# Down-projection operands made and split during the gate and up products and kept in DRAM as two parts

## Chip, cores and metric

The kernel runs on one core of one Trainium2 chip. The metric is the time of one execution in microseconds on the device: the median of the runs of the kernel before is 2508.19 us (3 runs, 2506.65 to 2509.33).

## The reference

Two transformer blocks follow each other on the same 1024 tokens of 1024 features, all in float32. The part that the change touches is the feed-forward at the end of each block, with 2816 hidden features:

```python
# first block
hn = rms_norm(h, ffn_pre_g)
ff = (jax.nn.silu(hn @ w_gate) * (hn @ w_up)) @ w_down
h = h + rms_norm(ff, ffn_post_g)
...
# second block
h = _rmsnorm(x, norm_ffn[l])
gate, up = jnp.split(h @ w_gu[l], 2, axis=-1)
x = x + (jax.nn.silu(gate) * up) @ w_down[l]
```

Ahead of it stand a convolution and sliding-window attention (first block), and three kinds of attention and a cross attention (second block). Nothing of those changes.

## The kernel before, in words

All activations are held feature-major: tiles of 128 features on the partitions by 512 tokens (a half of the sequence) in the columns. A float32 product is made of three matmuls (`mm3`, L530 to L535): each operand is split into a rounded part `hi` (a cast on ACT) and a low part `lo = x - hi` (a subtraction on POOL or DVE), and hi*hi, hi*lo and lo*hi are summed in PSUM. Weights come from DRAM as one stream of 128x512 pieces; `Weights.quarter` (L147) loads one with four feature tiles of one output column, and `Weights.parted` (L157) splits it with a cast on ACT (L162) and a subtraction on POOL, or on DVE where it is told so (L163).

**Gate and up** (`gated`, L1285). The 22 hidden tiles are taken one after the other; for each, the gate and the up tile of both halves of the tokens come from seven products (Winograd's form of Strassen's algorithm) instead of eight: 7 products x 4 feature tiles x 3 matmuls = 84 matmuls. I call this one hidden tile. For the seven, the weights are subtracted from each other on DVE (`difference`, L166) and split seven times. DVE and ACT take the products out of PSUM; silu(gate) is ACT L1300, the row scale after it POOL L1301, and `store` (L1304) multiplies the up part by it on DVE and sends the float32 tile to DRAM (`zff`, one 256 KB store for each half). The first hidden tiles (4 in the first block, 2 in the second: `NPRE`) are taken product by product, the other 18 + 20 = 38 in a main loop.

**Down** (`lower`, L1373). The hidden tiles are the inner dimension. They are taken in three chunks (`CHUNKS`) of 8, 8 and 6 tiles, and each chunk is once more done with seven products: its inner halves are its first and its last 4 (or 3) tiles, k and k + n, and its token halves are the rows. A chunk has seven stages, `stage` (L1415); each makes the operands of one product (4 or 3 tiles of 512 tokens) and the weights of four pairs of output tiles, and one stage later its 4 x 4 x 3 = 48 (or 36) matmuls run. The operands are x11 and x21 (tile k of the first and the second half of the tokens), x12 and x22 (tile k + n of them), and the sums s1 = x21 + x22, s2 = x11 - s1, s3 = x11 - x21, s4 = x12 + s2. So `seven` loads 4 tiles for each k from `zff`, makes the four sums on DVE (`vec`, L1398) and splits all seven with `parted` (L1391): cast on ACT (L422), subtraction on POOL, or on DVE for k = 1 and 3 (`XDVE`; both L423). Loads from `zff` are issued after `mark`, the last but one store.

**What sets the order.** Each engine works through its own instructions in the order in which a scheduler, at build time, put them; SP's queue (nearly all loads and stores) and POOL's few DMAs are in order too. Tiles come from rings of buffers (`BUFS`): whoever fills a buffer waits until its last reader is done. The rings that matter here are `wq` (weights as they come), `wt` (their differences), `whi` and `wlo` (their parts), `ge` (tiles of the gate stage) and `x` (58 buffers: the operands of the gate products, and then those of the down products).

## Time and profile before

| | |
|---|---|
| median of the runs | 2508.19 us (2506.65 to 2509.33) |
| span of the profiled execution | 2505.9 us |
| what lies around the span | not shown by the page; the median is 2.3 us above the span |
| PE matmul busy | 2372.9 us, 95% of the span, 11892 matmuls |
| DVE, POOL, ACT busy | 1894.8 us (76%), 1641.7 us (66%), 1015.9 us (41%) |
| gate and up products | about 445 to 908 us and 1805 to 2240 us |
| down products | about 908 to 1155 us and 2240 to 2491 us |

Busy time is the union of an engine's instructions. Matmuls overlap each other, so one that lasts 0.39 us starts about 0.23 us after the one before it. Idle time is named by the instruction that came after it and by what that waited for.

### The profile page before, as it was taken

Reading aid. Unit: us, or ns where it says so; the run is one execution under the profiler, and the core shown is the slowest. Engines: PE = TensorE matmul, PEld = TensorE weight load, DVE = VectorE, ACT = ScalarE, POOL = GpSimd, SP = SyncE. Lnnn points to the kernel's source line nnn. Section 1 sums busy time; section 2 is a strip of 40 time slices with the busy share of each in tenths; the row PEclk is TensorE's granted clock in tenths of the full one; section 3 lists DMA queues with packets and bytes.
Section 4 is the critical chain, followed back from the end, with each engine's and each line's share of the span. In section 5 each row is a group of like instructions: output and inputs, shape, how many; then the busy total and the mean of one; then the engine's idle time right before and its main releaser. Section 6 shows DMA issues by size and latency. Waiting matters only on the chain.

```text
span 2505.9 us, 34363 instructions
## 1 busy us (share of the span) xinstructions
PE 2372.9 (95%) x11892; PEld 1908.6 (76%) x11892; DVE 1894.8 (76%) x2784; ACT 1015.9 (41%) x2088; POOL 1641.7 (66%) x1194
## 2 busy tenths in 40 slices
PE   8788999889999999998999999999999999998987
PEld 7666777668888877776878778888878888876766
DVE  7989768999555589999443465676799555579988
ACT  5344754533232243435444353544533222334433
POOL 4657557998766669877522334164489666668885
PEclk9888999999999999999999999999999999999998
DMA  4211126423232233232653448113213222253221
GB/s 144 76 34 34 39 81 213 148 72 118 86 104 80 88 123 105 86 121 95 205 154 113 146 121 280 39 51 95 89 59 105 80 76 88 85 190 103 77 73 67
DMA packets 141421, 259.62 MB, mean 104 GB/s; under 512 B 15712, under 2 KB 28352, under 8 KB 141248
## 3 DMA queue, kind: packets, MB, share of 16 engines
q1 hardware_dynamic: 134512, 235.34, 28.9%
q0 software_dynamic: 6448, 21.91, 2.8%
q8 instruction: 94, 1.54, 0.3%
q14 instruction: 79, 0.65, 0.1%
q10 hardware_dynamic: 288, 0.18, 0.0%
HBM read 188.42 MB, written 68.94 MB: 103 GB/s over the span
## 4 chain that ended last, share of the span: by engine, by line
PE 59%; DVE 14%; issue 3%; POOL 2%; ACT 1%; DMA 1%; SPq 0%; DVEq 0%; POOLq 0%; ACTq 0%
PE p L535 10%; PE p L533 10%; PE p L534 10%; PE mm L533 4%; PE mm L534 4%; PE mm L535 4%; DVE s L1398 2%; PE tp L584 2%; PE low L535 2%; PE low L534 2%; PE low L533 2%; DVE ff L423 2%; DVE wt L174 1%; PE lo L1885 1%; DVE ffacc L1398 1%
## 5 line engine op out<-in xcount | busy, mean ns | idle before, releaser
L163 POOL TENSOR_TENSOR xlo<-wt,xhi 128x512 fp32r<-128x512 f32 (+1 forms) x230 | 358.1, 1575 | 31.7 <-ACT xhi L162 24.0
L163 POOL TENSOR_TENSOR xlo<-wraw,xhi 128x512 fp32r<-128x512 f32 (+1 forms) x204 | 321.3, 1588 | 26.5 <-ACT xhi L162 24.1
L140 POOL TENSOR_TENSOR wlo<-wraw,whi 128x512 fp32r<-128x512 f32 x144 | 205.7, 1437 | 142.1 <-ACT whi L139 120.5
L533 PE MATMUL p<-s,xhi 128*128 128x512 f32 x704 | 278.3, 396 | 1.3 <-DVE u L1292 1.0
L535 PE MATMUL p<-s,xlo 128*128 128x512 f32 x704 | 277.7, 396 | 0.9 <-POOL xlo L163 0.9
L534 PE MATMUL p<-s,xhi 128*128 128x512 f32 x704 | 278.0, 395 | 0.0
L535 PE MATMUL low<-ff,xlo 128*128 128x512 f32 (+1 forms) x628 | 252.9, 403 | 25.2 <-POOL xlo L163 25.2
L534 PE MATMUL low<-ff,xhi 128*128 128x512 f32 (+1 forms) x628 | 251.2, 400 | 6.6 <-DVE ff L423 4.5
L533 PE MATMUL low<-ff,xhi 128*128 128x512 f32 (+1 forms) x628 | 250.5, 400 | 5.5 <-DVE u L1398 3.7
L1301 POOL TENSOR_TENSOR g<-g,rbc 128x512 f32<-128x512 f32 x82 | 116.4, 1421 | 188.2 <-ACT g L1300 188.2
L1300 ACT ACTIVATE g<-g 128x512 f32<-128x512 f32 x82 | 51.9, 633 | 422.2 <-DVE g L1299 413.6
L533 PE MATMUL p<-x,xhi 128*128 128x512 f32 x528 | 210.2, 398 | 5.6 <-ACT early L1300 4.9
L535 PE MATMUL p<-x,xlo 128*128 128x512 f32 x528 | 210.6, 399 | 1.1 <-POOL xlo L163 1.1
L534 PE MATMUL p<-x,xhi 128*128 128x512 f32 x528 | 210.0, 398 | 0.1
L162 ACT CAST xhi<-wt 128x512 fp32r<-128x512 f32 (+1 forms) x248 | 142.6, 606 | 144.0 <-DVE wt L174 103.7
L535 PEld LDWEIGHTS low<-ff,xlo 128*128 128x128 f32 x628 | 122.1, 194 | 59.3 <-POOL xlo L163 32.7
L533 PEld LDWEIGHTS p<-s,xhi 128*128 128x128 f32 x704 | 132.8, 189 | 33.4 <-ACT xhi L162 1.4
L535 PEld LDWEIGHTS p<-s,xlo 128*128 128x128 f32 x704 | 132.6, 188 | 32.6 <-POOL xlo L163 1.8
L534 PEld LDWEIGHTS p<-s,xhi 128*128 128x128 f32 x704 | 132.9, 189 | 31.2
L534 PEld LDWEIGHTS low<-ff,xhi 128*128 128x128 f32 x628 | 122.3, 195 | 35.9 <-DVE ff L423 5.8
L533 PEld LDWEIGHTS low<-ff,xhi 128*128 128x128 f32 x628 | 122.1, 194 | 34.3 <-issue 4.2
L162 ACT CAST xhi<-wraw 128x512 fp32r<-128x512 f32 (+1 forms) x228 | 129.6, 599 | 36.4 <-POOL xlo L163 13.5
(446 smaller groups left out, 6445.9 us busy)
## 6 DMA issues: line engine op xcount, KB each, us to landing
wraw<-wstream SPq DMA_DIRECT2D x408, 256.0 KB, 3.0
ff<-zff SPq DMA_DIRECT2D x88, 256.0 KB, 3.5
zff<-up SPq DMA_DIRECT2D x76, 256.0 KB, 2.0
res<-zres SPq DMA_DIRECT2D x48, 256.0 KB, 5.4
x<-xT SPq DMA_DIRECT2D x32, 256.0 KB, 5.4
zres<-res SPq DMA_DIRECT2D x32, 256.0 KB, 2.0
lqk<-zl POOLq DMA_DIRECT2D x16, 512.0 KB, 6.3
wraw<-wstream SPq DMA_DIRECT2D x32, 192.0 KB, 3.1
```

The costliest lines, as they stand in the source:

```text
L140: self.last_part = nc.gpsimd.tensor_tensor(lo, raw, hi.bitcast(F32), op=ALU.subtract)
L162: self.nc.scalar.copy(hi, raw)
L163: ins = (eng or self.nc.gpsimd).tensor_tensor(lo, raw, hi.bitcast(F32), op=ALU.subtract)
L174: self.nc.vector.tensor_tensor(t, a, b, op=ALU.subtract)
L423: return (eng or nc.gpsimd).tensor_tensor(lo, src, f32(hi), op=ALU.subtract)
L533: nc.tensor.matmul(ps, lhsT=ah, rhs=bh, start=first and i == 0, stop=False)
L534: nc.tensor.matmul(ps, lhsT=ah, rhs=bl, start=False, stop=False)
L535: nc.tensor.matmul(ps, lhsT=al, rhs=bh, start=False, stop=last and i == n - 1)
L584: nc.tensor.transpose(ps[:, tsl(j)], pr[:, c0 + (g + j) * P:][:, :P], ident)
L1300: nc.scalar.activation(t, t, AF.Silu)
L1301: nc.gpsimd.tensor_tensor(t, t, rb_[h], op=ALU.mult)
L1398: nc.vector.tensor_tensor(out, x_, y_, op=op)
```

## The change

In `gated`, a hidden tile is no longer stored as it is. Tiles 2m and 2m + 1 of both token halves are now x11, x21, x12, x22 of one operand index m, so that the inner halves of a chunk are its even and its odd tiles; `quarter` takes its weight tiles in steps of two accordingly. As soon as the four are there, the sums are made on DVE in the gate stage. Each of the seven operands is then put to DRAM in two parts (`put`): ACT rounds it (`hi`), and SP stores that; ACT rounds it once more with the sign turned (`lo` = -hi), a DMA from POOL's queue adds the operand to it in place (`accum_op`, `lo` = x - hi), and SP stores that. `some` lets one such put follow after each of four of the seven products of a hidden tile in the main loop; what is left follows the last product. `lower` then only loads the two parts, two 256 KB loads for each operand tile, and no longer subtracts, adds or splits activations. Weights are subtracted and split as before, but their parts have rings of their own (`phi`, `plo`: 6 buffers each); `ge` goes from 9 to 13 buffers, `wt` from 6 to 5, `wq` from 8 to 7. The loads are now issued after the last weight load of the gate stage (`W.last`). Comments are gone too, and line numbers shift: the rounding of weights is L161 in place of L162, their subtraction L162 in place of L163.

```diff
-BUFS = {'v': 39, ..., 'ge': 9, 'wt': 6, 'wq': 8, ...}
+BUFS = {'phi': 6, 'plo': 6, 'hi': 2, 'lo': 3, 'fs': 2, 'v': 39, ..., 'ge': 13, 'wt': 5, 'wq': 7, ...}
...
-    def quarter(self, mat, k, c0, n=4):
+    def quarter(self, mat, k, c0, n=4, step=1):
...
-        self.order += [(mat, k + i, c0) for i in range(n)] + [None] * (4 - n)
+        self.order += [(mat, k + i * step, c0) for i in range(n)] + [None] * (4 - n)
...
-        hi = self.pool.tile([P, 512], F32R, tag="whi", name=f"xhi{self.made}", bufs=BUFS["whi"])[:, :w]
-        lo = self.pool.tile([P, 512], F32R, tag="wlo", name=f"xlo{self.made}", bufs=BUFS["wlo"])[:, :w]
+        hi = self.pool.tile([P, 512], F32R, tag="phi", name=f"xhi{self.made}", bufs=BUFS["phi"])[:, :w]
+        lo = self.pool.tile([P, 512], F32R, tag="plo", name=f"xlo{self.made}", bufs=BUFS["plo"])[:, :w]
...
+    OPERANDS = ("x11", "s1", "s2", "s3", "x22", "s4", "x12")
...
-        z = dp.tile([NFF, 2, P, HALF], F32, name=nm("zff"))
+        z = dp.tile([NFF // 2, 7, 2, P, HALF], F32, name=nm("zff"))
+        f, due = {}, []
+
+        def put(name, m, t):
+            hi = slot("hi", HALF)("hi", F32R)
+            nc.scalar.copy(hi, t)
+            nc.sync.dma_start(z[m, OPERANDS.index(name), 0], f32(hi))
+            lo = slot("lo", HALF)("lo", F32R)
+            nc.scalar.activation(lo, t, AF.Copy, scale=-1.0)
+            nc.gpsimd.dma_start(lo, t, accum_op=ALU.add)
+            nc.sync.dma_start(z[m, OPERANDS.index(name), 1], f32(lo))
+
+        def ready(i, h, t):
+            f[i, h] = t
+            m = i // 2
+            if i % 2 == 0:
+                if h == 0:
+                    due.append(lambda: put("x11", m, t))
+                return
+            due.append(lambda: put(("x12", "x22")[h], m, t))
+            if any((j, g) not in f for j in (i - 1, i) for g in (0, 1)):
+                return
+            x11, x21, x12, x22 = (f.pop((j, g)) for j in (i - 1, i) for g in (0, 1))
...
+            due.extend((s3, s1, s2, s4))
+
+        def some(n=1):
+            for _ in range(min(n, len(due))):
+                due.pop(0)()
...
         def store(i, h, up_, g):
             nc.vector.tensor_tensor(up_, up_, g, op=ALU.mult)
-            return nc.sync.dma_start(z[i, h], up_)
+            ready(i, h, up_)
...
+            some()
             ps = product("p2", pair, sums)
...
+            some()
             ps = product("p6", pair, sums)
...
+            some()
             ps = product("p5", pair, sums)
...
+            some()
             ps = product("p3", pair, sums)
             with tc.high_priority(offset=EVP):
-                last = store(i, b, tt(ge("up1"), ps, u2, ALU.add), g1)
-            if i == NFF - 2:
-                mark = last
-        return z, mark
+                store(i, b, tt(u2, ps, u2, ALU.add), g1)
+        some(len(due))
+        return z, W.last
...
-        def load(k, h):
-            t = xt("ff")
-            with tc.issue_after(mark.ins):
-                late[0] = nc.sync.dma_start(t, z[k, h])
-            return t
-
-        def parted(t, k):
-            hi, lo = xt("ff", F32R), xt("ff", F32R)
-            ins = split(hi, lo, t, nc.vector if k in XDVE else nc.gpsimd)
-            if k not in XDVE:
-                late[1] = ins
+        def operand(name, m):
+            hi, lo = xt("ff", F32R), xt("ff", F32R)
+            for t, part in ((hi, 0), (lo, 1)):
+                with tc.issue_after(mark.ins):
+                    late[0] = nc.sync.dma_start(f32(t), z[m, OPERANDS.index(name), part])
             return hi, lo
...
-                return [W.quarter(down, n0 + n * row, (2 * q + col) * P, n) for q in Q4]
+                return [W.quarter(down, n0 + row, (2 * q + col) * P, n, 2) for q in Q4]
 
-            def stage(ws, xs, evac, done=None):
-                parts = [parted(t, k) for k, t in enumerate(xs)]
+            def stage(ws, name, evac, done=None):
+                parts = [operand(name, n0 // 2 + k) for k in K]
...
-            x21 = [load(n0 + k, 1) for k in K]
-            x22 = [load(n0 + n + k, 1) for k in K]
-            s1 = [xt("s1") for k in K]
-            for k in K:
-                vec(s1[k], x21[k], x22[k])
-            yield stage(t, s1, ev5)
+            yield stage(t, "s1", ev5)
...
```

**Where instructions move.** POOL in the main loop of the first block's gate stage. `xlo` are low parts of weights, `g` the scale after silu, `oh` a table that is loaded once. Before:

```order
L163 TENSOR_TENSOR xlo_5975<-wt_5972,xhi_5974 128x512
L1301 TENSOR_TENSOR g_810_5800<-g_810_5800,rbc_4462 128x512
L163 TENSOR_TENSOR xlo_5996<-wt_5993,xhi_5995 128x512
L163 TENSOR_TENSOR xlo_6015<-wt_5970,xhi_6014 128x512
L163 TENSOR_TENSOR xlo_6037<-wt_6034,xhi_6036 128x512
L163 TENSOR_TENSOR xlo_6061<-wraw_5966,xhi_6060 128x512
L1301 TENSOR_TENSOR g_818_5892<-g_818_5892,rbc_4618 128x512
```

The same place now; `lo` is the low part of an operand, and L1301 is now the DMA that adds to it:

```order
L1351 TENSOR_TENSOR g_832_5753<-g_832_5753,rbc_4462 128x512
L162 TENSOR_TENSOR xlo_5930<-wraw_5927,xhi_5929 128x512
L1301 DMA lo_6141<-up_798_5462 128x512
L1301 DMA lo_6198<-s_885_6193 128x512
L162 TENSOR_TENSOR xlo_5967<-wt_5964,xhi_5966 128x512
L1301 DMA lo_6252<-s_892_6247 128x512
L162 TENSOR_TENSOR xlo_5988<-wt_5985,xhi_5987 128x512
L162 TENSOR_TENSOR xlo_6014<-wt_5962,xhi_6013 128x512
L1351 TENSOR_TENSOR g_845_5862<-g_845_5862,rbc_4618 128x512
```

Between the same two `g` POOL now has three DMA issues beside the four subtractions, each of which waits for ACT to have written its `lo`.

SP's queue in the same place. Before, two stores for each hidden tile (L1306) stand between the weight loads (L113; `z` is the table of the relative bias):

```order
L113 DMA wraw_6834<-wstream 128x512
L113 DMA wraw_6836<-wstream 128x512
L1153 DMA z_3441<-z2s_6273 128x512
L113 DMA wraw_6949<-wstream 128x512
...
L113 DMA wraw_6970<-wstream 128x512
L1306 DMA zff_4111<-up_882_6464 128x512
L1306 DMA zff_4111<-up_878_6418 128x512
L113 DMA wraw_6994<-wstream 128x512
```

Now:

```order
L112 DMA wraw_6304<-wstream 128x512
L112 DMA wraw_6335<-wstream 128x512
L1298 DMA zff_4111<-hi_6195 128x512
L112 DMA wraw_6337<-wstream 128x512
L1298 DMA zff_4111<-hi_6249 128x512
L1302 DMA zff_4111<-lo_6141 128x512
L1302 DMA zff_4111<-lo_6198 128x512
L1302 DMA zff_4111<-lo_6252 128x512
L112 DMA wraw_6531<-wstream 128x512
L1298 DMA zff_4111<-hi_6296 128x512
L112 DMA wraw_6560<-wstream 128x512
L1302 DMA zff_4111<-lo_6299 128x512
```

Stores of low parts (L1302), each of which waits for POOL's adding DMA to land, now stand directly ahead of weight loads in the same queue.

POOL in the first block's down stage. `ff` are low parts of operands, `ffacc` sums of the output. Before:

```order
L163 TENSOR_TENSOR xlo_9002<-wraw_8737,xhi_9001 128x512
L423 TENSOR_TENSOR ff_8986<-ff_8641,ff_8985 128x512
L163 TENSOR_TENSOR xlo_9006<-wraw_8739,xhi_9005 128x512
L423 TENSOR_TENSOR ff_8994<-ff_8645,ff_8993 128x512
L163 TENSOR_TENSOR xlo_9010<-wraw_8741,xhi_9009 128x512
L423 TENSOR_TENSOR ff_9098<-ff_8761,ff_9097 128x512
L423 TENSOR_TENSOR ff_9106<-ff_8765,ff_9105 128x512
L423 TENSOR_TENSOR ff_9198<-s_1157_8769,ff_9197 128x512
```

Now:

```order
L162 TENSOR_TENSOR xlo_9160<-wraw_9135,xhi_9159 128x512
L162 TENSOR_TENSOR xlo_9164<-wraw_9137,xhi_9163 128x512
L162 TENSOR_TENSOR xlo_9168<-wraw_9139,xhi_9167 128x512
L162 TENSOR_TENSOR xlo_9264<-wt_9239,xhi_9263 128x512
L162 TENSOR_TENSOR xlo_9268<-wt_9241,xhi_9267 128x512
L162 TENSOR_TENSOR xlo_9272<-wt_9243,xhi_9271 128x512
```

Only the weights' subtractions are left between the sums of the output.

## Rows read from the trace of the kernel before

**Rows 1.** First page, engine totals: busy us, share of the span, instructions.
```profile
PE 2372.9 (95%) x11892; PEld 1908.6 (76%) x11892; DVE 1894.8 (76%) x2784; ACT 1015.9 (41%) x2088; POOL 1641.7 (66%) x1194
```
**Rows 2.** Windows: gate main loops (first two), then the two down stages.
```profile
core 0: us, PE busy (x) PEld busy (x) DVE busy (x) ACT busy (x) POOL busy (x), PEclk, DMA share, GB/s
640.00:880.00 240.00, 240.00 (x1043) 194.63 (x1042) 136.75 (x182) 70.76 (x131) 161.88 (x114) 1.00 0.27 88
1920.00:2240.00 320.00, 320.00 (x1384) 259.51 (x1384) 197.13 (x251) 93.03 (x169) 224.75 (x152) 1.00 0.28 94
908.00:1155.00 247.00, 226.03 (x945) 179.17 (x944) 233.82 (x251) 105.25 (x198) 204.91 (x134) 0.97 0.30 96
2240.00:2452.00 212.00, 193.49 (x795) 152.73 (x794) 204.83 (x216) 82.46 (x154) 181.28 (x113) 0.96 0.30 98
```
**Rows 3.** Groups of PE by line, down stage of the first block: busy, mean ns | idle before.
```profile
L535 PE MATMUL low<-ff,xlo 128*128 128x512 f32 x307 | 124.9, 407 | 13.0 <-POOL xlo L163 13.0
L533 PE MATMUL low<-ff,xhi 128*128 128x512 f32 x308 | 124.5, 404 | 1.4 <-DVE u L1398 1.4
L534 PE MATMUL low<-ff,xhi 128*128 128x512 f32 x308 | 124.1, 403 | 2.1 <-POOL ff L423 2.1
L494 PE MATMUL bc<-constr,sum 128*64 128x1 f32 x16 | 1.0, 247 | 4.4 <-DVE sum L448 4.4
```
**Rows 4.** The same groups, down stage of the second block up to its tail.
```profile
L535 PE MATMUL low<-ff,xlo 128*128 128x512 f32 x263 | 107.1, 407 | 12.2 <-POOL xlo L163 12.1
L534 PE MATMUL low<-ff,xhi 128*128 128x512 f32 x264 | 107.0, 405 | 4.5 <-DVE ff L423 4.5
L533 PE MATMUL low<-ff,xhi 128*128 128x512 f32 x264 | 105.6, 403 | 1.8 <-DVE res L1398 1.8
```
**Rows 5.** Waits in the first block's down stage: us in total, times, longest.
```profile
ACT xhi L162 <- DVE wt L174: 52.7, 14, 7.9
ACT ff L422 <- DVE s L1398: 41.8, 18, 6.2
```
**Rows 6.** Groups of POOL and of DVE, first block's down stage.
```profile
L423 POOL TENSOR_TENSOR ff<-ff,ff 128x512 fp32r<-128x512 f32 x22 | 37.8, 1728 | 1.9 <-issue 1.9
L423 POOL TENSOR_TENSOR ff<-s,ff 128x512 fp32r<-128x512 f32 x18 | 27.9, 1555 | 14.7 <-ACT ff L422 14.7
...
L423 DVE TENSOR_TENSOR ff<-ff,ff 128x512 fp32r<-128x512 f32 x18 | 27.3, 1523 | 0.0
L423 DVE TENSOR_TENSOR ff<-s,ff 128x512 fp32r<-128x512 f32 x15 | 19.5, 1299 | 1.4 <-ACT ff L422 1.4
```
**Rows 7.** Groups of POOL, DVE and ACT, main loop of the first gate stage (640 to 880 us).
```profile
L1301 POOL TENSOR_TENSOR g<-g,rbc 128x512 f32<-128x512 f32 x25 | 32.5, 1299 | 72.2 <-ACT g L1300 72.2
L1145 POOL DMA_DIRECT2D oh<-oh x4 | 2.3, 582 | 0.0
...
L1305 DVE TENSOR_TENSOR up<-up,g 128x512 f32<-128x512 f32 x24 | 30.1, 1293 | 0.4
...
L162 ACT CAST xhi<-wt 128x512 fp32r<-128x512 f32 x50 | 28.5, 615 | 0.0
```
**Rows 8.** Windows at the start of the main loops, first and second block.
```profile
560.00:640.00 80.00, 80.00 (x346) 64.71 (x346) 69.47 (x78) 25.65 (x47) 66.22 (x41) 1.00 0.36 119
1840.00:1920.00 80.00, 80.00 (x349) 64.92 (x348) 73.27 (x69) 24.59 (x44) 69.77 (x46) 1.00 0.25 83
```
**Rows 9.** DMA issues of the whole span: times, size of one, median us to landing.
```profile
zff<-up SPq DMA_DIRECT2D x76, 256.0 KB, 2.0
oh<-oh POOLq DMA_DIRECT2D x2, 256.0 KB, 3.2
aq<-zfq POOLq DMA_DIRECT2D x4, 512.0 KB, 9.2
```
**Rows 10.** Windows with the most DMA traffic outside the stages above.
```profile
375.00:405.00 30.00, 30.00 (x154) 24.29 (x154) 20.60 (x33) 11.57 (x23) 19.10 (x18) 1.00 0.72 244
1500.00:1550.00 50.00, 50.00 (x269) 41.27 (x268) 24.63 (x54) 14.34 (x31) 26.77 (x26) 1.00 0.96 329
```

More of the change, by code (lines that the diff above doesn't have):

```diff
@@ L30 @@
 BYDVE = (3,)
-XDVE = (1, 3)
 POSTPOOL = (0, 1, 2, 4, 5, 6)
@@ L1288, in gated, with fs, s3, s1 @@
         b = 1 - a
-        z = dp.tile([NFF, 2, P, HALF], F32, name=nm("zff"))
+        z = dp.tile([NFF // 2, 7, 2, P, HALF], F32, name=nm("zff"))
[8 more added lines that the diff above has]
+            nc.sync.dma_start(z[m, OPERANDS.index(name), 1], f32(lo))
+        def fs(name):
+            return slot("fs", HALF)(name)
+        def ready(i, h, t):
[9 more added lines that the diff above has]
+            x11, x21, x12, x22 = (f.pop((j, g)) for j in (i - 1, i) for g in (0, 1))
+            s = {}
+            def s3():
+                d = tt(fs("s3"), x11, x21, ALU.subtract)
+                put("s3", m, d)
+            def s1():
+                tt(x21, x21, x22, ALU.add)
+                put("s1", m, x21)
+            def s2():
+                s[2] = tt(fs("s2"), x11, x21, ALU.subtract)
+                put("s2", m, s[2])
+            def s4():
+                put("s4", m, tt(fs("s4"), s[2], x12, ALU.add))
+            due.extend((s3, s1, s2, s4))
+        def some(n=1):
+            for _ in range(min(n, len(due))):
+                due.pop(0)()
         def tt(out, x_, y_, op):
@@ L1479, in seven @@
             b11 = weights(0, 0)
-            x11 = [load(n0 + k, 0) for k in K]
-            yield stage(b11, x11, ev1)
+            yield stage(b11, "x11", ev1)
             b12 = weights(0, 1)
             t = [W.difference(b12[q], b11[q]) for q in Q4]
-            x21 = [load(n0 + k, 1) for k in K]
-            x22 = [load(n0 + n + k, 1) for k in K]
-            s1 = [xt("s1") for k in K]
-            for k in K:
-                vec(s1[k], x21[k], x22[k])
-            yield stage(t, s1, ev5)
+            yield stage(t, "s1", ev5)
             b22 = weights(1, 1)
-            for k in K:
-                vec(s1[k], x11[k], s1[k], ALU.subtract)
             t2 = [W.difference(b22[q], t[q], t[q]) for q in Q4]
-            yield stage(t2, s1, ev6)
-            for k in K:
-                vec(x11[k], x11[k], x21[k], ALU.subtract)
-            yield stage([W.difference(b22[q], b12[q], b12[q]) for q in Q4], x11, ev7, 3)
-            x12 = [load(n0 + n + k, 0) for k in K]
+            yield stage(t2, "s2", ev6)
+            yield stage([W.difference(b22[q], b12[q], b12[q]) for q in Q4], "s3", ev7, 3)
             b21 = weights(1, 0)
@@ L1502, in seven @@
                     before_last()
-            yield stage([W.difference(t2[q], b21[q], t2[q]) for q in Q4], x22,
+            yield stage([W.difference(t2[q], b21[q], t2[q]) for q in Q4], "x22",
                         adder(2, ALU.subtract), 2)
-            for k in K:
-                vec(s1[k], s1[k], x12[k])
-            part = stage(b22, s1, adder(1), 1)
+            part = stage(b22, "s4", adder(1), 1)
             def first_half():
@@ L1515, in seven @@
             tail = end and not fresh_all and TAIL
-            last = stage(b21, x12, adder(0), -1 if tail else 0)
+            last = stage(b21, "x12", adder(0), -1 if tail else 0)
             if end and ahead:
```

3 lines of the change are left out of this document (2 added, 1 removed).

## Prediction, made before the change was run

> **What bounds the kernel now.** The first page comes first: PE's matmuls are busy for 95% of the span [rows 1], so an engine beside PE matters only where PE waits for it. The windows show where that is. In the main loops of the two gate stages PE is never idle, and 1384 matmuls take 320.00 us: 0.2312 us each [rows 2]. At that rate the 945 matmuls of the first down stage would take 218.5 us; they take 247, 28.5 more. The 795 of the second one, up to its tail, would take 183.8 us and take 212, 28.2 more. So 56.7 us are lost in the two down stages, and this is the stretch that the change relieves.
>
> What PE waits for there is in its groups by line [rows 3, 4]. In the first block: 13.0 us for POOL's low part of a weight, 2.1 for POOL's low part of an operand, 1.4 for a sum on DVE, 4.4 for a sum of squares at the end; in the second 12.1 (12.2 with all), 4.5 for DVE's low part of an operand, 1.8 for a sum. Together 39.4 us of idling. The other 17 us are mostly the clock, which falls after such waits: the granted clock is 0.97 and 0.96 of full speed over these windows, 0.03 x 247 + 0.04 x 212 = 15.9 us, while it is 1.00 in the gate loops [rows 2].
>
> Most waits are for weights, which the change leaves where they are. But why they are late is one step further back: POOL and DVE are busy for 83% and 95% of the first down window [rows 2], ACT waits 52.7 us for differences of weights that DVE has not made yet and 41.8 for sums of operands [rows 5], and POOL's `xlo` comes after ACT's `xhi`. DVE's backlog, then POOL's, reaches PE.
>
> **What goes from the down stages.** Each layer has 11 operand indices x 7 = 77 splits: 77 casts on ACT, 42 subtractions on POOL (k = 0 and 2; some 1.65 us each [rows 6]: 69 us) and 35 on DVE (some 1.4 us [rows 6]: 49 us), and 44 sums on DVE (priced at 1.29, the two-input DVE row of the gate stage [rows 7]: 57 us). DVE is left with 234 - 106 = 128 us of the 247, POOL with 205 - 69 = 136. Neither is then close to full. I take all waits for `xlo` and for `ff` to end: 13.0 + 12.1 + 2.1 + 4.5 = 31.7 us. The clock's part goes with them in proportion, 31.7 / 39.4 x 15.9 = 12.8 us. **Down: -44.5 us.** The sums of squares and of the output stay.
>
> **What the down stages get.** Two loads in place of one load and a split for each operand: 154 loads of 256 KB a layer instead of 44, and no engine between DRAM and PE. They fill buffers of the `x` ring, 58 deep, some six stages ahead. In the first layer, with 48 weight loads (a quarter of a MB or less), 16 residual loads and 8 weight pieces for the next block, that is some 58 MB in 219 us, 266 GB/s; the stage moves 96 GB/s now [rows 2]. The traffic has been as high as 329 GB/s over 50 us with PE fully busy [rows 10], so I expect it to pass, but with less room: weights stand in SP's queue behind operand loads, `wq` and `wt` have one buffer fewer, and the parts of weights have 6 buffers each instead of sharing 8. New waits lie between 0 and the 31.7 us that I took off; with DVE and POOL half free I take a quarter. **+8 us.**
>
> **What the gate stages get.** A hidden tile has 84 matmuls, 19.4 us. The window of 240 us holds 1043 / 84 = 12.4 of them [rows 2]. For each, on average, come 3.5 puts and two sums:
> - POOL: 161.88 / 12.4 = 13.0 us, plus 3.5 DMA issues. An adding DMA is in no row; the nearest is POOL's issue of a plain DMA, 0.58 us [rows 7]. 15.1 us of 19.4.
> - DVE: 136.75 / 12.4 = 11.0, plus 2 x 1.29 = 13.6 us.
> - ACT: 70.76 / 12.4 = 5.7, plus 7 casts of 0.62 [rows 7] = 10.0 us.
> - SP: 5 more stores, issue time alone; a store lands in 2.0 us [rows 9].
> - Transfers: 5 stores and 3.5 additions of 256 KB are 2.2 MB more in 19.4 us, 115 GB/s beside the 88 at a share of 0.27 [rows 2]; the share goes to some 0.6, or 0.77 if an addition counts twice.
>
> So every engine stays under PE's 19.4 us, and that spare time is the cover; where it is gone is the start of the loops. There DVE is busy for 69.5 and 73.3 of 80 us [rows 8], and four hidden tiles would add 10.7: 80.2 and 84.0. The lower bound is nothing, the upper is the first rival's. I take 4 us a layer, the overflow in the fuller of the two windows. **+8 us.** The last puts run beside the first down chunk, and only the last chunk reads them: nothing. Ordering loads after the last weight load, and even and odd tiles instead of halves, cost nothing: the host lays out the weights, and the transfers keep their size.
>
> **Sum.** -44.5 + 8 + 8 = -28.5 us. It is made from one profiled execution with a span of 2505.9 us, 2.3 under the median of 2508.2; I apply it to the median: 2479.7, **2480 us**.
>
> **Rivals.** *A, POOL becomes the bound of the gate stages (slower).* POOL has 19.4 - 13.0 = 6.4 us to spare for each hidden tile, and it is not all usable: its order is fixed, and it stands 72.2 us in 240 before the scale after silu [rows 7], 5.8 us a tile. If 1 us of that cannot be filled, 3.5 issues fit as long as one takes under 1.54 us. If an issue has to sit out a DVE operation, 0.58 + 1.29 = 1.87 us [rows 7], POOL is 1.15 us over in each of 38 tiles: +44 in place of my +8, 2516 us, and 133 us more for each further us of an issue. Against it: the plain issues took 0.58 us beside a busy DVE, and POOL arrives later at silu, so most of the standing goes.
>
> The Trainium skill, page "SBUF — State Buffer", sections "SBUF: two separate sides" and "A bandwidth-pool intuition that's wrong (but worth ruling out)", speaks against the change here: POOL writes the descriptors of its own DMAs itself, a DVE copy in a mode that takes the port both share locks it out, and a DMA of some 620 ns then took some 3100. By that figure an issue would cost 3.1 us and POOL would need 13.0 + 3.5 x 3.1 = 23.9 us a tile, an estimate of 4.5 x 38 = 170 us lost from that page. The page says it of copies and casts, not of two-input operations, which are most of DVE's work in this loop; the trace's four issues agree with its undisturbed figure.
>
> *B, the addition lands late (slower).* A low part passes ACT's cast (0.62), POOL's issue (0.58), the landing L, SP's store and its landing (some 0.4 + 2.0), 3.6 + L in all, through a ring of three, and the store blocks SP's queue meanwhile, weight loads behind it. 3.5 of them take 3.5 / 3 x (3.6 + L) us a tile. POOL's DMAs landed in 3.2 us for 256 KB and 9.2 at most for 512 KB [rows 9]; from L = 13 the ring is slower than PE, at 14 it costs 1.1 us x 38 = 42 in place of my 8: 2514 us, and more if the puts bunch.
>
> *C, the change does not do what it says for weights.* PE waits for `xlo`, and those splits stay, with fewer buffers. If only half of the down term comes off, with the new waits in it: 2508.2 - 22.3 + 8 = 2494 us.
>
> *D, the down stages become bound by transfers.* At 244 GB/s, a rate that the trace shows at a share of 0.72 [rows 10], 58 MB take 238 us instead of 219: 19 us return in the first layer and some 15 in the second, which has no reloads: 2508.2 - 44.5 + 34 + 8 = 2506 us.
>
> **How the numbers follow.** My forecast, 2462 to 2496 by its own bounds (the whole down term less little, or twice the new costs), gets 0.47; C 0.18; A 0.17; B 0.09; D 0.09. About 0.2%, 5 us, is what a measurement of this kernel can tell from no change. Forecast and C are faster, but for a corner of C (0.64 with a little of D); D and the edges of C and A fall within 0.2% (0.09); A, B and a part of D are slower (0.27). The range holds the forecast, C, D and the near parts of A and B: 2458 to 2530 us.
>
> **What would show it.** Right: in the down windows the granted clock is 1.00, PE's idle before `low` falls from the 35 us of [rows 3, 4] (without the sums of squares) to under 10, DVE is busy for half; the gate loops keep 0.231 us a matmul; POOL's adding DMA is issued in about 0.6 us and lands in 3 to 6. Wrong: gaps before p products behind POOL's `xlo` or `g` (A), stores of `lo` in SP's queue waiting over 10 us and weights late behind them (B), `xlo` still at the head of PE's waits in the down stages (C), or PE there waiting for a DMA of `ff` at a share near 1 (D).

## The result, and the profile after

The changed kernel takes **2548.8 us** (median of 4 runs, 2546.8 to 2551.8) against 2508.7 of the kernel before on the same chip: a ratio of **1.0161, 95% interval 1.0146 to 1.0175**. It is 40 us slower, where 28 us faster was forecast, and outside the range. The profiled execution has a span of 2549.7 us, 43.8 more than the one shown of before.

Where that went is read by stretches, from the first to the last matmul of the gate products (`p`) and of the down products (`low`); the last column is an experiment told below, the change without its addition.

| stretch, us | before | after | difference | without the addition |
|---|---|---|---|---|
| start to the end of the first gate stage | 908.0 | 934.8 | +26.8 | 909.6 |
| first down stage | 247.0 | 231.0 | -16.0 | 214.8 |
| second block up to its gate stage | 650.1 | 665.4 | +15.3 | 665.9 |
| second gate stage | 435.5 | 481.3 | +45.8 | 434.4 |
| second down stage | 250.6 | 223.7 | -26.9 | 216.1 |
| rest | 14.6 | 13.4 | -1.2 | 13.7 |

So the two down stages gave 42.9 us, where 36.5 net were forecast, and the two gate stages cost 72.6. Windows of the changed kernel, the four of [rows 2] with the down stages at their new places:

```profile
core 0: us, PE busy (x) PEld busy (x) DVE busy (x) ACT busy (x) POOL busy (x), PEclk, DMA share, GB/s
640.00:880.00 240.00, 231.16 (x983) 183.63 (x983) 201.64 (x196) 109.49 (x205) 184.17 (x149) 0.99 0.70 194
1920.00:2240.00 320.00, 300.72 (x1250) 236.73 (x1250) 293.05 (x255) 135.21 (x253) 228.86 (x188) 0.98 0.63 176
...
935.00:1166.00 231.00, 219.15 (x941) 175.42 (x941) 132.66 (x181) 75.42 (x144) 131.94 (x105) 0.97 0.76 260
...
2312.00:2536.00 224.00, 219.50 (x997) 178.48 (x996) 142.85 (x201) 68.93 (x131) 127.89 (x99) 0.98 0.72 246
```

In the first down stage DVE and POOL are busy for 57% each (95% and 83% before), and PE's groups there, against [rows 3], show no wait for POOL but a new one for transfers:

```profile
L533 PE MATMUL low<-ff,xhi 128*128 128x512 f32 x308 | 122.2, 398 | 1.8 <-DMA ff<-zff 1.8
L534 PE MATMUL low<-ff,xlo 128*128 128x512 f32 x308 | 121.5, 398 | 1.1 <-POOL xlo L162 0.8 <-DVE xlo L162 0.4
L532 PE MATMUL low<-ff,xhi 128*128 128x512 f32 x308 | 120.2, 398 | 8.9 <-DMA ff<-zff 8.9
```

The gate loops were at 1043 and 1384 matmuls with PE never idle; now 983 and 1250 pass in the same time. PE's waits in the two gate stages (428 to 935 us, then 1831 to 2312):

```profile
PE p L534 <- POOL xlo L162: 20.4, 25, 2.5
PE p L532 <- ACT xhi L161: 7.7, 5, 2.6
...
PE p L534 <- POOL xlo L162: 23.0, 17, 4.0
PE p L532 <- ACT xhi L161: 8.5, 6, 3.0
```

These short waits on the parts of weights point to POOL. But POOL is busy for 184.17 us of 240 and 228.86 of 320 (161.88 and 224.75 before), so it is far from full. What has changed most is DVE: from 197.13 to 293.05 us of 320, for fewer matmuls. Two of its groups in the second gate loop before:

```profile
L1299 DVE TENSOR_TENSOR g<-g,rbc 128x512 f32<-128x512 f32 x33 | 23.7, 719 | 1.1
...
L174 DVE TENSOR_TENSOR wt<-wraw,wt 128x512 f32<-128x512 f32 x15 | 12.1, 809 | 0.0
```

Its groups there after the change, and POOL's in the first loop:

```profile
L173 DVE TENSOR_TENSOR wt<-wraw,wt 128x512 f32<-128x512 f32 x15 | 69.6, 4638 | 5.4 <-DMA zff<-hi 3.1 <-ACT xhi L161 2.3
L1349 DVE TENSOR_TENSOR g<-g,rbc 128x512 f32<-128x512 f32 x30 | 60.8, 2027 | 1.0
L1355 DVE TENSOR_TENSOR up<-up,g 128x512 f32<-128x512 f32 x15 | 26.7, 1781 | 0.0
...
L1342 DVE TENSOR_TENSOR u<-u,p 128x512 f32<-128x512 f32 x30 | 20.4, 680 | 0.9
```
```profile
L162 POOL TENSOR_TENSOR xlo<-wt,xhi 128x512 fp32r<-128x512 f32 x45 | 73.8, 1751 | 5.5 <-DMA zff<-hi 3.6 <-ACT xhi L161 1.8
...
L1351 POOL TENSOR_TENSOR g<-g,rbc 128x512 f32<-128x512 f32 x23 | 33.9, 1474 | 24.7 <-ACT g L1350 24.7
L1301 POOL DMA_DIRECT2D lo<-s x18 | 22.8, 1283 | 0.0
L1301 POOL DMA_DIRECT2D lo<-u x12 | 11.5, 962 | 11.8 <-ACT lo L1300 11.0 <-issue 0.6
L1301 POOL DMA_DIRECT2D lo<-up x12 | 10.7, 890 | 13.2 <-DVE wt L173 6.2 <-ACT lo L1300 4.2 <-ACT hi L1297 2.8
```

Read the means. DVE's operations with one input from PSUM (`u<-u,p`) still take 680 ns. Those with both inputs from SBUF, the difference of weights and the row scale, went from 809 and 719 ns to 4638 and 2027. The record of an adding DMA's issue on POOL lasts 0.89 to 1.28 us, not 0.58. (These records overlap their neighbours: counted from the end of the instruction before it, an adding DMA takes 0.87 us of POOL in this loop, and the plain copy of experiment 2 0.55.) POOL's standing before `g`, 72.2 us in [rows 7], is down to 24.7. The timeline of one place, first DVE, then POOL, shows how the two belong together (columns: start, duration):

```profile
709.31 0.69 DVE L1342 TENSOR_TENSOR g<-u,p 128x512 f32<-128x512 f32 x1 [0.30 <-DMA zff<-lo]
710.03 5.32 DVE L1349 TENSOR_TENSOR g<-g,rbc 128x512 f32<-128x512 f32 x1
715.27 0.68 DVE L173 TENSOR_TENSOR wt<-wraw,wraw 128x512 f32<-128x512 f32 x1
```
```profile
708.30 0.88 POOL L1301 DMA_DIRECT2D lo<-up  x1
708.89 1.19 POOL L1301 DMA_DIRECT2D lo<-s  x1
709.46 1.93 POOL L162 TENSOR_TENSOR xlo<-wt,xhi 128x512 fp32r<-128x512 f32 x1
710.70 1.53 POOL L1301 DMA_DIRECT2D lo<-s  x1
711.32 3.47 POOL L162 TENSOR_TENSOR xlo<-wt,xhi 128x512 fp32r<-128x512 f32 x2
716.10 1.29 POOL L1351 TENSOR_TENSOR g<-g,rbc 128x512 f32<-128x512 f32 x1 [1.31 <-ACT g L1350]
```

A row scale of 0.69 us stands for 5.32, as long as POOL goes from one instruction to the next without a pause, and ends 0.56 us after POOL's last one, in its pause. Of DVE operations over 3 us the gate stages have 25 (2 before). The next silu, on ACT, starts only when this one is over.

That such stalls reach PE shows in the second loop. Seven differences of weights take 7.0 to 7.1 us each there, and 20.2 to 20.4 us after the start of each PE has just stood 1.6 us for POOL's low part of a weight: the first one starts at 1961.19, and PE goes on at 1981.36. Over both gate stages, against the run without the addition, PE is idle for 44 us more (70.8 in place of 26.6), and for as many matmuls busy for 28 us more, at a granted clock of 0.97 in both in place of 0.98 and 1.00. That is the 72 us.

Which DVE operations stand can be read from all 19 traces of this case, over the gate stages and for operations of 128x512 float32. The 5665 with one input from PSUM took 0.67 to 0.69 us each, whatever POOL did. The 2207 with both inputs from SBUF that no instruction of POOL's overlapped took 0.67 to 0.70. The 6279 others of these took up to 10.1 us, 1.46 in the mean. Beside one operation of POOL's the longest took 1.81 us, and only such were held up as began after POOL's; the 151 beside one issue of a DMA alone, adding or plain, stayed at 0.67 to 0.70. So a DVE operation with both inputs from SBUF waits for POOL's subtractions and scales, and not for its DMA issues.

### The profile page after: what moved, and what is told of

Read it like the earlier page. It is cut to its first block, busy times and chain, and to the rows that moved or that the text cites. A ratio compares the mean times of both kernels' runs of the same rounds, so it can differ in the third digit from the quotient of the medians.

```text
span 2549.7 us, 35644 instructions
## 1 busy us (share of the span) xinstructions
PE 2394.1 (94%) x11892; PEld 1911.9 (75%) x11892; DVE 1904.9 (75%) x2714; ACT 1096.0 (43%) x2242; POOL 1561.6 (61%) x1264
## 3 DMA queue, kind: packets, MB, share of 16 engines
q8 instruction: 94, 1.54, 0.2%
## 5 line engine op out<-in xcount | busy, mean ns | idle before, releaser
L162 POOL TENSOR_TENSOR xlo<-wt,xhi 128x512 fp32r<-128x512 f32 (+1 forms) x230 | 360.3, 1651 | 136.6 <-ACT xhi L161 116.1
L162 POOL TENSOR_TENSOR xlo<-wraw,xhi 128x512 fp32r<-128x512 f32 (+1 forms) x204 | 298.6, 1541 | 28.7 <-ACT xhi L161 10.8
L534 PE MATMUL p<-s,xlo 128*128 128x512 f32 x704 | 284.5, 406 | 26.1 <-POOL xlo L162 26.1
L532 PE MATMUL p<-s,xhi 128*128 128x512 f32 x704 | 283.3, 402 | 11.6 <-ACT xhi L161 7.1
L533 PE MATMUL p<-s,xhi 128*128 128x512 f32 x704 | 281.4, 400 | 0.0
L532 PE MATMUL low<-ff,xhi 128*128 128x512 f32 (+1 forms) x628 | 244.3, 394 | 13.4 <-DMA ff<-zff 8.9
L533 PE MATMUL low<-ff,xhi 128*128 128x512 f32 (+1 forms) x628 | 246.7, 394 | 1.8 <-DMA ff<-zff 1.8
L534 PE MATMUL low<-ff,xlo 128*128 128x512 f32 (+1 forms) x628 | 245.5, 393 | 1.1 <-POOL xlo L162 0.8
L161 ACT CAST xhi<-wt 128x512 fp32r<-128x512 f32 (+1 forms) x248 | 144.9, 605 | 209.6 <-DVE wt L173 170.8
L1351 POOL TENSOR_TENSOR g<-g,rbc 128x512 f32<-128x512 f32 x82 | 122.5, 1496 | 101.5 <-ACT g L1350 101.4
L173 DVE TENSOR_TENSOR wt<-wraw,wt 128x512 f32<-128x512 f32 (+1 forms) x74 | 145.1, 1962 | 19.7 <-POOL xlo L162 8.4
L1349 DVE TENSOR_TENSOR g<-g,rbc 128x512 f32<-128x512 f32 x82 | 151.6, 1852 | 2.3
L532 PEld LDWEIGHTS low<-ff,xhi 128*128 128x128 f32 x628 | 119.2, 190 | 41.5 <-ACT xhi L161 13.4
L161 ACT CAST xhi<-wraw 128x512 fp32r<-128x512 f32 (+1 forms) x228 | 131.4, 600 | 37.3 <-DMA wraw<-wstream 18.7
```

Of the source, the lines that this page charges most:

```text
L161: self.nc.scalar.copy(hi, raw)
L162: ins = (eng or self.nc.gpsimd).tensor_tensor(lo, raw, hi.bitcast(F32), op=ALU.subtract)
L173: self.nc.vector.tensor_tensor(t, a, b, op=ALU.subtract)
L532: nc.tensor.matmul(ps, lhsT=ah, rhs=bh, start=first and i == 0, stop=False)
L533: nc.tensor.matmul(ps, lhsT=ah, rhs=bl, start=False, stop=False)
L534: nc.tensor.matmul(ps, lhsT=al, rhs=bh, start=False, stop=last and i == n - 1)
```

## The experiments

Lines without a number belong to `put`; medians of before are those of the same chip. "Gates" is the first gate stage plus the second, first to last `p` matmul: 898.7 us before, 987.0 after.

**1. Without the addition.** `-nc.gpsimd.dma_start(lo, t, accum_op=ALU.add)`

> Leaves out the adding DMA: the stored low part is -hi instead of x - hi. Everything else of the change stays. Four theories of the 88 us that the two gate stages lost. Starved DVE: DVE's two-input operations (the row scale, the differences of weights, the product with silu) stand while POOL runs one instruction behind another, and the adding DMAs have filled the pauses that POOL had. Then the pauses return, the mean of the row scale on DVE falls from 2175 ns to under 1000, the two gate stages lose less than 20 us against the kernel before: 2465 to 2485 us. Adding itself: the addition is slow or blocks something as an addition; same result here. Traffic (5 more stores of 256 KB a hidden tile, and the addition): most of it stays, 2530 to 2550 us. Added work (2 sums on DVE and 7 casts on ACT a hidden tile): nothing comes back, 2540 to 2550 us.

2455.3 us against 2507.1 (0.979, 0.9774 to 0.9806): 94 us less than the change, 52 less than before, 10 under the lower end that was expected. Gates 915.0 (16 more than before, since the first one starts 16 us earlier with the 56 matmuls told of below; it ends 1.6 us later), no waits in the down stages. The last column of the table above is this run. Stores, casts and DVE's sums are all still there, and the loops are back at 1043 and 1385 matmuls, so those cost nothing by themselves in the loops. DVE's row scale takes 1093 ns in the first loop, not quite under 1000.

```profile
640.00:880.00 240.00, 240.00 (x1043) 194.62 (x1042) 179.94 (x211) 117.89 (x224) 160.42 (x116) 1.00 0.47 164
1920.00:2240.00 320.00, 320.00 (x1385) 259.70 (x1384) 239.68 (x284) 152.59 (x285) 201.64 (x144) 1.00 0.51 176
```

**2. A plain copy in its place.** `+nc.gpsimd.dma_start(lo, t.bitcast(F32R))`

> The adding DMA becomes a plain copy of the same tile from the same queue of POOL (the stored low part is x instead of x - hi); the order of every engine stays the same. Starved DVE: POOL issues as many DMAs in the same places, so DVE is as starved: the row scale on DVE stays over 1700 ns, 2535 to 2555 us. Adding itself: 2465 to 2490 us. Traffic: the copy moves the same bytes or a little less, 2535 to 2550 us.

2477.0 us (0.9883, 0.9861 to 0.9904): 72 of the 94 us belong to the adding as such, 22 to a DMA on POOL's queue (18 of them in the gate stages). That as many issues starve DVE as much is refuted (the row scale takes 1427 ns). This run has the issue price that the prediction used. The copies are issued in half the time:

```profile
L1301 POOL DMA_DIRECT2D lo<-s x18 | 9.9, 553 | 0.0
L1301 POOL DMA_DIRECT2D lo<-up x12 | 7.2, 600 | 12.5 <-ACT lo L1300 6.3 <-DVE wt L173 6.2
```

**3. The copy from ACT's queue.** `+nc.scalar.dma_start(f32(lo), t)`

> The same copy, but issued from ACT's queue right behind the second cast (the stored low part is x instead of x - hi): traffic and stores as with the copy from POOL's queue, no DMA on POOL. Starved DVE: the row scale on DVE under 1000 ns, 2465 to 2490 us. Traffic: 2535 to 2550 us. Added work: 2535 to 2550 us.

2453.6 us (0.979, 0.9775 to 0.9805), 11 under the expected range, gates 914.9: moving the same bytes costs nothing, at a DMA share of 0.60 and 0.63 in the loops' windows.

**4. A subtraction on POOL.** `+nc.gpsimd.tensor_tensor(lo, t, f32(hi), op=ALU.subtract)` for the second cast and the addition

> The second cast and the adding DMA are replaced by a subtraction on POOL, which computes the same. POOL then works 13.0 + 3.5 x 1.6 = 18.6 us of the 19.4 us of a hidden tile and issues no DMA there. Starved DVE: what counts is that POOL has no pauses, not that it issues DMAs: the row scale on DVE stays over 1500 ns, and the kernel is as slow as the change or slower, 2535 to 2600 us. If it is the issue of a DMA on POOL that stops DVE (and not a dense POOL): the row scale under 1100 ns, 2475 to 2510 us.

2531.5 us (1.0102, 1.0087 to 1.0117), between the two expected ranges, gates 985.1: nearly as slow as the change without any DMA on POOL, but in another way. POOL is full (218.96 of 240 us), the row scale takes 1137 ns, and only 2 of DVE's operations in the gate stages take over 3 us. So a POOL without pauses is not enough for those long stalls; that part of the theory fell.

**5. and 6. Adding DMAs alone, and copies alone, on the kernel before:** 3.5 for each hidden tile, from `rb_[b]` into a ring of three. The scheduler did not leave them there: in experiments 5 to 10 the added operations stand in the first part of each loop, up to 11 a hidden tile (the full adding DMAs in tiles 2 to 13, counted from 0, of 22, the subtractions in 2 to 14), and none after.

```diff
+            lo = slot("lo", HALF)("lo", F32R)
+            nc.scalar.activation(lo, rb_[b], AF.Copy, scale=-1.0)
+            nc.gpsimd.dma_start(lo, rb_[b], accum_op=ALU.add)
```

> The kernel before, with nothing of the change but 3.5 adding DMAs (and the cast ahead of each) for each hidden tile of the two gate loops, 133 in all, from a tile that is always there into a ring of three; their results are read by nobody, no store waits for them. Two theories of why adding costs 72 us more than copying. Issue: the adding DMA holds POOL for 0.9 to 1.3 us in place of 0.57, POOL's subtraction behind it takes some 2.2 us, and DVE's two-input operations wait for both; then it costs time here too, 2525 to 2570 us, DVE's row scale over 1200 ns in place of 713. Landing: the addition lands in 6.4 us instead of 3.8, so stores of low parts block SP's queue and the ring; here nothing waits for it but the ring: 2505 to 2515 us.

> The same with plain copies in place of the adding DMAs. Issue: 0.57 us of POOL each, which fits into the pauses; 2505 to 2520 us. Landing: 2505 to 2512 us.

2543.2 us with adding DMAs (1.0148, 1.0128 to 1.0169), 2515.3 with copies (1.0037, 1.0024 to 1.005), against 2506.0: +37 and +9. No store waits here, so late landing is not needed for the loss. DVE's row scale takes 1157 ns in the first loop, a little under what was expected, and 1538 in the second.

**7. and 8. Half the rows, half the columns** (`lo[0:64, :]`, and `lo[:, 0:256]`, source alike)

> The adding DMAs alone on the kernel before, each over 64 of the 128 partitions (half the rows of 2 KB, half the bytes). If POOL's hold goes with the rows that an adding DMA has to be written out for, the issue takes 0.5 to 0.65 us instead of 1.16 and the kernel 2508 to 2525 us. If it is a fixed price of an adding DMA: 1.0 us and more, 2530 to 2550 us.

> The same with all 128 partitions and 256 of the 512 columns (the same number of rows, half the bytes). If the hold goes with the rows: issue 1.0 to 1.2 us, 2530 to 2550 us. If it goes with the bytes: 0.5 to 0.65 us, 2508 to 2525 us.

2539.5 us (1.0125, 1.0109 to 1.0142) and 2537.3 (1.0117, 1.0101 to 1.0134). The hold is neither by rows nor by bytes: counted from the end of the instruction before it, an adding DMA takes 0.83 to 0.85 us of POOL alone, 0.80 over half the rows and 0.84 to 0.85 over half the columns, and a copy alone 0.52 to 0.53. POOL's issues in the full, the half-row and the half-column run:

```profile
L1308 POOL DMA_DIRECT2D lo<-rbc x133 | 154.5, 1198 | 1.9 <-ACT xhi L162 1.0 <-ACT lo L1307 0.7
```
```profile
L1308 POOL DMA_DIRECT2D lo<-rbc x133 | 155.4, 1331 | 2.7 <-ACT lo L1307 1.8 <-ACT xhi L162 0.9
```
```profile
L1308 POOL DMA_DIRECT2D lo<-rbc x133 | 152.8, 1217 | 8.3 <-ACT lo L1307 5.7 <-PE p L534 2.7
```

**9. and 10. Every second adding DMA only; and a subtraction on POOL in the place of each**

> The adding DMAs alone on the kernel before, full size, but only every second one (66 in place of 133); the casts stay. With the run of half the rows it compares half the bytes in as many DMAs with half the bytes in half as many. If the price is per adding DMA: half the loss of 37 us, 2515 to 2528 us. If the price comes from their density (two or three in a row that shut DVE out): most of it goes, 2505 to 2515 us.

> On the kernel before, in the place of each of the 133 adding DMAs a subtraction on POOL (some 1.6 us each, more of POOL's time than the 1.2 us of an adding DMA's issue). If an adding DMA costs through the time it takes on POOL: more than the 37 us of the adding DMAs, 2545 to 2570 us. If it costs mainly through what it does to DVE's operations and to the subtraction behind it: less, 2510 to 2535 us, with fewer operations of DVE over 3 us than the 41 there.

2525.5 us against 2508.8 (1.0073, 1.0052 to 1.0093): half as many cost half. But they are not half as dense: the scheduler put them into the first seven tiles of either loop, 4.8 a tile in place of some 6.5, so the theory of density was hardly tested. With subtractions 2573.5 (1.0266, 1.0248 to 1.0284): +65, more than the adding DMAs and 3.5 above the expected range, with 5 operations of DVE over 3 us in the gate stages where these have 37. The time that POOL is given counts, then, but it is not all: half of the adding DMAs take 67 x 0.85 = 57 us of POOL and cost 17, the 133 copies take 71 and cost 9.

**11. and 12. More work on DVE alone.** After these runs a new theory was formed. POOL's operations and DVE's operations with both inputs from SBUF keep each other out, so the sum of both has to fit into PE's 19.4 us. Each at what it takes alone, 1.29 and 0.69 us: before, 9 and 8 of them, 11.6 + 5.5 = 17.1 us for each hidden tile. The adding DMAs counted as POOL's operations in it, which the traces do not bear out (no DVE operation stood beside a DMA issue alone). The test adds seven sums on DVE to the kernel before, one behind each product, first with one input from PSUM, then with none.

```diff
+            nc.vector.tensor_tensor(slot("lo", HALF)("lo"), ps, rb_[a], op=ALU.add)
```

(`rb_[b]` for `ps` in the second.)

> On the kernel before, seven more sums on DVE for each hidden tile of the gate loops (one behind each product, results read by nobody), with one input from PSUM (the product) and one from SBUF. Two theories of what fills up in a hidden tile of 19.4 us. Shared port: POOL's operations (1.3 us each when alone) and DVE's operations with both inputs from SBUF (0.69 us when alone) exclude each other, and it is their sum that must stay under 19.4: 9 x 1.29 + 8 x 0.69 = 17.1 us before, 11.6 + 2.1 to 4.2 + 6.9 = 20.6 to 22.7 with the change. Operations with a PSUM input do not count: 17.1 still, 2505 to 2515 us. Engine time: DVE has 11.0 + 7 x 0.69 = 15.8 of 19.4 us, 2505 to 2515 us.

> The same seven sums on DVE in the same places, with both inputs from SBUF. No work is added on POOL, no DMA, no wait. Shared port: 17.1 + 7 x 0.69 = 21.9 us of 19.4, 2530 to 2580 us, and POOL's subtractions lengthen or start later while POOL is not full. Engine time: DVE's 15.8 us of 19.4 as in the run with a PSUM input, 2505 to 2515 us, or a little more where a sum takes 1.3 us (11.0 + 9.1 = 20.1, over 19.4 by 0.7 us in 38 tiles: up to 2535 us).

2519.4 us (1.0049, 1.0032 to 1.0066) and **2620.3 us** (1.0449, 1.0429 to 1.0469) against 2508.3. The same number of operations, on the same engine, put in at the same places of the program: +11 and +112. First the run with PSUM, then the one without, in the second gate loop and by the added group in the first:

```profile
1920.00:2240.00 320.00, 320.00 (x1384) 259.34 (x1383) 294.57 (x371) 93.27 (x169) 218.67 (x152) 1.00 0.27 87
...
L1305 DVE TENSOR_TENSOR lo<-p,rbc 128x512 f32<-128x512 f32 x85 | 57.9, 681 | 1.0 <-ACT s L1354 1.0
```
```profile
1920.00:2240.00 320.00, 283.33 (x1156) 225.41 (x1155) 310.79 (x361) 81.53 (x144) 213.21 (x132) 0.94 0.22 71
...
L1305 DVE TENSOR_TENSOR lo<-rbc,rbc 128x512 f32<-128x512 f32 x85 | 78.9, 961 | 0.0
```

DVE is busy for 294.57 us of 320 in the first, and PE loses nothing there; a DVE at 92% is no bound. Its rise by 11 us is 5 between the first down stage and the second gate stage and 7 in the second down stage, where no sum was added; the first gate stage ends when it did before, and the second lasts as long. The second run lost more than the expected upper end of 2580, 110 us of it in the gate stages.

The two do not differ in their inputs alone. A sum with the product as input has to wait for it, and these stand at seven or eight a hidden tile over the whole loop. The sums that wait for nothing were drawn forward by the scheduler: 10 to 19 in each of nine tiles early in a loop, next to none after. By an estimate from these rows that is 11.0 + 15 x 0.69 = 21.4 us of work for DVE in 19.4, with no more waiting for POOL than before, 2 us too much in 18 tiles: 36 of the 110 us by engine time alone. The mean of 961 ns in place of 681 is the part that comes with the inputs.

**13. to 17. Versions that split elsewhere.** A version without an adding DMA: each operand is split in the gate stage by a subtraction on POOL or DVE, or stored in float32 and split in the down stage as before ("late").

```diff
+            if HOW[name] == "late":
+                nc.sync.dma_start(z[m, OPERANDS.index(name), 0], t)
+                return
...
+            (nc.gpsimd if HOW[name] == "pool" else nc.vector).tensor_tensor(
+                lo, t, f32(hi), op=ALU.subtract)
```

> The change without its split: the gate stages make the sums and store all seven operands in float32, 3.5 stores a hidden tile, and the down stages split them as the kernel before did (casts on ACT, subtractions on POOL for k = 0 and 2, on DVE for k = 1 and 3). No DMA on POOL in the gate stages, 77 splits back in each down stage, 44 sums less on DVE there than before. By the theory that POOL's DMAs alone cost the gate stages their time, these take what they take without the addition, and DVE in a down stage has 128 + 49 us of work in 247: down stages lose under 10 us each against the 215 without splits: 2455 to 2480 us. If it was the splits and not the sums that made the down stages late: 2490 to 2505 us.

> The change with the low parts subtracted instead of added by a DMA, and the second cast gone: on POOL for x11, s1 and s3 (1.5 a hidden tile, 13.0 + 1.5 x 1.6 = 15.4 us of 19.4), on DVE for the other four (2 a hidden tile, 15 + 2 x 1.4 = 17.9 us of 19.4). If engine time is what counts, both fit: 2455 to 2480 us. If DVE starves beside a POOL that is rarely idle: 2500 to 2540 us.

> Four of the seven operands are split in the gate stage by subtraction (x11 and s3 on POOL, s1 and s2 on DVE), three are stored in float32 and split in the down stages (x22, s4, x12). POOL has 13 + 1.6 us of the 19.4 of a hidden tile, DVE 15 + 1.4; a down stage gets 33 subtractions in place of 77. Theory of engine time: between the two kernels that put all splits on one side, each of which lost some 40 us, half of it or less on either side: 2460 to 2480 us. If either side loses as much with half the work (a late order, not a full engine): 2485 to 2500 us.

> Two operands split in the gate stage, both on POOL (x11 and s1: 13 + 1.6 us), DVE has the sums alone; five are split in the down stages, 55 subtractions. Engine time: the gate stages lose under 5 us each, the down stages some 10 each: 2465 to 2485 us.

> Five of seven operands split in the gate stage (x11 and s3 on POOL, s1, s2 and s4 on DVE), x22 and x12 in the down stages. By what four and seven early ones gave (gate stages 490 and 438, or 503 and 442 us; down stages 225 and 225, or 215 and 221): 2480 to 2490 us, no better than four early; if the best lies between them: 2470 to 2480 us.

| split in the gate stage | median, us | ratio (interval) | gates | both down stages |
|---|---|---|---|---|
| none | 2492.6 | 0.994 (0.9924 to 0.9957) | 915.8 | 469.3 |
| two: POOL 2 | 2498.9 | 0.9973 (0.9955 to 0.999) | 921.9 | 465.0 |
| four: POOL 2, DVE 2 | 2486.9 | 0.9915 (0.989 to 0.9939) | 927.5 | 450.0 |
| **five: POOL 2, DVE 3** | **2477.1** | **0.9882 (0.9863 to 0.9902)** | 931.7 | 439.3 |
| seven: POOL 3, DVE 4 | 2488.1 | 0.9927 (0.9909 to 0.9944) | 945.6 | 435.4 |

The versions with none, two and four came out 7 to 14 us above the upper end expected by engine time, the one with seven 8 us above. None and four fell into the range of the other theory named there, seven between its two ranges. With none, the gate stages are as fast as without the addition and the down stages take 469 us, where before took 498 and a kernel without splits there 431: of the 67 us, 28 went with the sums on DVE, the rest with the splits. **Five** is the fastest complete kernel, 31.7 us under before and 72 under the change.

## Why the prediction was wrong

**Down, -44.5 + 8: right in kind, and near in size because two errors cancel.** The two stages gave 42.9 us net, 36.5 forecast. In experiment 1, where all waits and the whole loss of clock went (granted 1.00), they gave 66.7: the relief was put 22 us too low, and what the change takes back of it, 23.8 us, 16 too low. The new wait for `ff` was 10.7 us, in the first stage alone, and is gone with the addition; rival D's bound by transfers did not show: in experiment 1 PE never waited there, at a share of 0.73.

**Gate, +8: wrong (72.6 measured), and this is the step.** "So every engine stays under PE's 19.4 us, and that spare time is the cover." By the windows, divided by their hidden tiles (983 / 84 = 11.7, 1250 / 84 = 14.9), POOL took 15.7 and 15.4 us (15.1 forecast), ACT 9.4 and 9.1 (10.0), and the transfers' share was 0.70 and 0.63 (0.6 to 0.77). Only DVE's term failed: 17.2 and 19.7 us, not 13.6, at two sums more as forecast. The two sums were even priced too high: 1.29 us each, where most took 0.68. What failed is the 11.0 us ahead of them. In it are eight operations with both inputs from SBUF for each hidden tile, at what they took beside a POOL that paused for 78 of 240 us ([rows 2]): the row scale 713 ns, 2175 and 2027 now. POOL's pauses were counted as spare for POOL and, unseen, for DVE as well. What such operations (of 128x512 float32) took above 0.68 us each, added up over both gate stages, goes with the loss:

| the change, with the low part made by | DVE's waiting, us | loss of both gate stages, us |
|---|---|---|
| nothing | 206 | 0 |
| a copy from ACT's queue | 209 | 0 |
| a copy from POOL's queue | 280 | 18 |
| a subtraction on POOL | 319 | 68 |
| an adding DMA (the change) | 338 | 72 |

(The loss is counted from the run without the addition, to the end of the first gate stage and over the second.) The waiting is not all: with subtractions POOL is also full itself. On the kernel before, adding DMAs bring DVE's waiting from 157 to 323 us and cost 37 us in the gate stages, subtractions to 283 and cost 63, with POOL busy for 312.49 of 320 us.

The price of the issue was wrong too: 0.58 us, from a plain DMA, where an adding one kept POOL for 0.87 us beyond the end of the instruction before it. With a plain copy the kernel takes 2477.0 us, and 2480 was forecast; that it comes so near is partly luck, since there the down stages gave 65 us, the gate stages cost 18, and the middle 20. And the right price alone would still have given no loss: 13.0 + 3.5 x 0.87 = 16.0 us of POOL is under 19.4.

The theory of experiment 11, that the sum of both engines has to fit into 19.4 us, does not hold as a bound. With five operands split early it is 17.1 + 2 x 0.69 for the sums + 1.29 + 1.5 x 0.69 for the splits = 20.8 us for each hidden tile, and still 1385 matmuls pass in the 320 us of the second loop's window with PE never idle, 19.4 us for a hidden tile. Its 13 us of loss lie at the starts of the loops (278 and 313 matmuls in the windows of [rows 8], 323 and 345 without the addition). For how much of its time one such operation shuts the other out was not measured.

Why does an adding DMA make DVE wait, if its issue does not hold DVE? The traces show how, though not why. In the five runs with adding DMAs, and in none of the other fourteen, POOL's next instruction often begins over 0.1 us before the running one has ended. In the change, a DVE operation that began during a subtraction or scale of POOL's was passed over (took more than 1.9 us) in 47 of the 51 cases where POOL's next instruction had begun by the end of that one, and in 2 of the other 178. Copies from POOL's queue, without such overlaps, still passed it over in 25 of 262 cases. Why POOL's instructions overlap after an adding DMA is open.

The Trainium skill, page "SBUF — State Buffer", section "SBUF: two separate sides", says that DVE and GpSimd share a pair of ports, that it is held for a whole instruction, and that a DVE operation with two SBUF inputs needs it against a GpSimd operation that reads SBUF. The prediction took from that page only that copies and casts lock out POOL's writing of descriptors, which the page does not say of two-input operations; it passed over that the same section names two inputs against POOL's own operations. The traces agree with it: 0.67 to 0.69 us with an input from PSUM, up to 1.81 beside one operation of POOL's with both from SBUF. The section speaks of the instruction that started first; here a waiting operation stood behind several, 5.32 us.

**Rival A** had the right stage, and POOL's issues as the cause, with a chance of 0.17 and 2516 us. Its own condition was not met (an issue over 1.54 us; it took 0.89 to 1.28), and the loss came nevertheless, since it counted POOL alone. The wait that it took from the page, POOL's issue behind a DVE operation, ran the other way: DVE waited, and for POOL's operations. **Rival B** fell: an addition landed in 3.9 to 6.4 us, not 13; alone, with no store behind it, it cost 37 us; no store of a low part held SP's queue for more than 5.8 us in the gate stages, and the subtraction of experiment 4, with no DMA to land, cost 68 us there. **Rival C** fell with the waits for `xlo`.

**The middle, +15.3: not in the prediction.** It is the same in the run without the addition: the first gate stage holds 56 matmuls more in the scheduler's new order, and the second block up to its gate stage takes 665 us instead of 650 for as many matmuls (4092 and 4088), at a granted clock of 0.98, not 1.00. Which move does it was not tried.

## What to carry to other kernels

Before work is moved beside a stage that has spare time, ask which engines hold each other up, here POOL's operations and DVE's with both inputs from SBUF. Spare time of one is then not spare time of the other, and holding each engine by itself against the bound, as was done here, says too little. Nor is the sum of both at their undisturbed durations a bound (20.8 us passed in 19.4); it is a warning. Which inputs an added operation reads is the first question: a sum with an input from PSUM took 681 ns, the same with both from SBUF 961. A cover is only as good as its price: take the duration that an operation has beside a busy neighbour, not the mean of a stage in which the neighbour pauses, and the price of the very instruction (an adding DMA), not of its nearest kin. And in a test with added work, look where the scheduler put it before comparing.

## What the hardware showed that was not expected

- The issue of an adding DMA from POOL's queue is recorded at 1.2 us alone and 0.89 to 1.28 in the first loop of the change, a plain copy's at 0.55 to 0.60. Beyond the end of the instruction before it, it took 0.80 to 0.87 us of POOL, at 256 KB as at 128 KB, over 64 partitions or 256 columns; the copy took 0.52 to 0.55. In the change it landed in 3.9 to 6.4 us, the copy in its place in 3.0 to 3.8; alone 4.1 and 2.4.
- In the five runs with adding DMAs POOL's next instruction often began over 0.1 us before the running one had ended, in the other fourteen never.
- A DVE operation with two SBUF inputs took 0.67 to 0.70 us beside an idle POOL or beside a single DMA issue of POOL's, up to 1.81 beside one operation of POOL's, and mostly 5 to 7 us, at most 10.1, behind a run of POOL's instructions, several of them, not one. With one input from PSUM it took 0.67 to 0.69 us throughout.
- 154 copies of 256 KB within SBUF, from ACT's queue, cost no time that shows: 2453.6 us with them, 2455.3 without.
